# Spreading the gate rows of an mLSTM over all partitions: a DMA from memory in place of a product with a one-hot

## The chip, the cores and the metric

The kernel runs on one core of one Trainium2 chip. The metric is the device time of one execution in microseconds (us); three executions of the kernel before took 1901.86, 1902.31 and 1902.44 us, so its median is 1902.31 us. The engines are TensorE (PE, with its weight loads listed apart as PEld), VectorE (DVE), ScalarE (ACT), GpSimd (POOL) and SyncE (SP), which here only calls transfers.

## The reference, cut to what matters

One layer works on 256 latent tokens and 256 context tokens of width 2048. After a modulated norm, one input projection makes the inputs of three mixers (a gated MLP, a two-way mLSTM, a pooling), an output projection follows, and then a retrieval network over 16,384 experts. The mLSTM has 4 heads of width 256 and runs once forward and once backward. For each head and direction it needs this, for every pair of a query token t and a key token s:

```
log_w = where(causal, b[t] - b[s] + i[s], -inf)
inter = b + m
m_t   = maximum(inter, log_w.max(-1))
w_prev = exp(inter - m_t)
s     = (q k^T) * exp(log_w - m_t)
num   = s v + w_prev * (C q);   den = s.sum(-1) + w_prev * (n q)
h     = num / maximum(|den|, exp(-m_t))
```

Two rows of 256 numbers per head and direction, one for the maximum and one for the weight of the earlier state, are functions of t alone. In the kernel the tokens s lie on the partitions and the tokens t along a row, so both rows have to stand on all 128 partitions before VectorE can combine them with the keys' own numbers.

## The kernel before, in words

All five instruction streams are written out in program order by one Python program; nothing reorders them later. The program walks through a list of units. A unit is half or a quarter of a block of weight columns: SP loads it as float32 (L277), ACT makes its high part `hi` (L295), DVE the rest `lo` (L305), and PE forms 24 products of 256 columns with them (12 of 512 where the tokens are the rows of the result). Three buffers each hold `hi` and `lo`, so ACT and DVE run at most three units ahead of PE. Between two units there stands one unit of the modulation weights (`araw`), which DVE alone multiplies and adds up (L452).

Everything else is written as generators that are resumed from a planner. The planner keeps a clock of PE time (`clock["t"]`, L357): each product adds its estimated time to it. A generator that yields a wait is resumed at the first pause after that wait, counted on this clock, but for the lane `main` not before the planner's own estimates of DVE's and ACT's time plus `MARG` (L327). So the place of a step among the units follows from the sum of the estimates ahead of it, and a product that goes away moves what stands behind it.

The generator `gen_heads` (L786) computes the mLSTM of the latent tokens, while PE works on the units of the o, v, p and u columns. For each head it calls `scores` (4 products, `pS`), and then for each direction `weights`, `products` (10 to 12 products, `num`) and `finish`; `norm` closes the head with a transpose on PE (`hT`, L872). In `weights` (L801) PE forms `bc1`: the transposed one-hot row `ident[:, row]`, read as 36 partitions by 128 columns, times the two rows of all heads in `rows3`, which gives the two rows of this head and direction on all partitions, 512 columns in one of three small PSUM buffers. DVE reads it in three steps (a maximum and a mask), ACT takes the exponential, DVE multiplies the queries by the second row (`qw`) and the weights by the scores (`sT`). The rows in `rows3` are made much earlier by `gen_gates` (L647).

When the last unit is done, `finish_mix` (L978) drains the generators: it runs the rest of `gen_heads` to its end. PE can go on with the output projection only after the last head's `hT` and the split of the mixers' results (`ysplit`). Transfers called by POOL are the row gathers of the retrieval network (L1372), which begin at 757 us.

Of the kernel before, what the change touches and what calls it, by code (L numbers as in the profile page):

```python
# [23 lines left out]
F32 = mybir.dt.float32  # L24
# [8 lines left out]
P = 128  # L33
D = 2048
KD = D // P
T = 256
# [3 lines left out]
HEADS = 4  # L40
# [142 lines left out]
def build(tc, a, stack, dbg=None):  # L183
    nc = tc.nc
    ten, pool, sync = nc.tensor, nc.gpsimd, nc.sync
# [11 lines left out]
    def dump(name, ap):  # L197
        if dbg is not None and name in dbg:
            sync.dma_start(dbg[name], ap)
# [9 lines left out]
    def sm_ps(name="sm"):  # L209
        return psp.tile([P, 512], F32, name=name, tag="sm", bufs=3)  # L210
# [9 lines left out]
    ident, iota, selb, iota_p = c1[:, 0:128], c1[:, 128:256], c1[:, 256:256 + BT], c1[:, 288:289]  # L220
# [126 lines left out]
    def mm(out, lhsT, rhs, start, stop, **kw):  # L347
        n = 1
        for x in rhs.shape[1:]:
            n *= x  # L350
        if rhs.dtype == F32:
            t = max(213.0, n * 4 / 2.4)
            if kw.get("tile_position") is not None:
                t /= 3.5
        else:
            t = max(107.0, n / 2.4)
        clock["t"] += t / 1000.0  # L357
        ten.matmul(out, lhsT, rhs, start=start, stop=stop, skip_group_check=True, **kw)  # L358
# [236 lines left out]
    ROWS = 36  # L595
    V = {}
# [30 lines left out]
    def big():  # L627
        return V["B"].tile([P, 2, T], F32, name="big", tag="t512", bufs=BIGB)


    def row_tile(name):
        return V["B"].tile([ROWS, 2, T], F32, name=name, tag="row", bufs=2)

    def prefix(dst, src, op):

        for r0, way in ((0, 1), (32, -1)):
            for i in range(2):
                d, x = dst[r0:r0 + 4, i, ::way], src[r0:r0 + 4, i, ::way]
                if op is OP.add:
                    vec.tensor_tensor_scan(d, ones[r0:r0 + 4, 0:1].to_broadcast([4, T]), x, 0.0, OP.mult, OP.add)  # L640
                else:
                    vec.tensor_tensor_scan(d, x, x, NEG, op, op)

    def gates_done(ps):
        vec.tensor_scalar(V["rowbuf"].rearrange("p i t -> p (i t)"), ps, vecs[:, V_BG:V_BG + 1], None, op0=OP.add)

    def gen_gates():  # L647
        B = V["B"]
        ig, fg = V["rowbuf"][0:ROWS], V["rowbuf"][64:64 + ROWS]
        e = big()  # L650
        act.activation(e[64:100], fg, AF.Abs)
        act.activation(e[64:100], e[64:100], AF.Exp, scale=-1.0)
        act.activation(e[64:100], e[64:100], AF.Ln, bias=1.0)

        lf = row_tile("lf")
        vec.memset(lf, 0.0)
        vec.scalar_tensor_tensor(lf, fg, 0.0, e[64:100], op0=OP.min, op1=OP.subtract)
        yield GY
        bc = B.tile([ROWS, 2, T], F32, name="bcum", tag="b1")
        vec.memset(bc, 0.0)  # L660
        prefix(bc, lf, OP.add)
        g = B.tile([ROWS, 2, T], F32, name="gexp", tag="b2")
        vec.tensor_tensor(g, ig, bc, op=OP.subtract)
        yield GY
        m = row_tile("pre")
        prefix(m, g, OP.max)
        col = B.tile([ROWS, 4], F32, name="gcol")
        vec.memset(col, 0.0)

        for r0, last in ((0, T - 1), (32, 0)):  # L670
            r = slice(r0, r0 + 4)
            vec.tensor_scalar(col[r, 0:1], m[r, 1, last:last + 1], 0.0, None, op0=OP.max)
            vec.tensor_tensor(col[r, 1:2], bc[r, 1, last:last + 1], col[r, 0:1], op=OP.add)
        vec.tensor_scalar(col[:, 2:3], col[:, 0:1], -1.0, None, op0=OP.mult)
        wk = row_tile("wk")
        vec.memset(wk, 0.0)
        yield GY
        act.activation(wk[:, 0], g[:, 1], AF.Exp, bias=col[:, 2:3])
        act.activation(wk[:, 1], g[:, 0], AF.Copy)
        rows3 = V["rows3"]  # L680
        vec.memset(rows3, 0.0)
        yield GY
        for r0 in (0, 32):
            r = slice(r0, r0 + 4)
            vec.tensor_scalar(rows3[r, 0], m[r, 0], col[r, 1:2], None, op0=OP.max)
            act.activation(rows3[r, 1], rows3[r, 0], AF.Exp, bias=col[r, 1:2], scale=-1.0)
            vec.tensor_tensor(rows3[r, 2], bc[r, 0], rows3[r, 0], op=OP.add)
            act.activation(rows3[r, 2], rows3[r, 2], AF.Exp, scale=-1.0)
        yield GY
        pt = sm_ps("gt")  # L690
        for i in range(2):
            for blk in range(2):
                n = 2 * i + blk
                ten.transpose(pt[:, n * ROWS:(n + 1) * ROWS], wk[:, i, blk * P:(blk + 1) * P],
                              ident[0:ROWS, 0:ROWS])
        for blk in range(2):
            n = 4 + blk
            ten.transpose(pt[:, n * ROWS:(n + 1) * ROWS], rows3[:, 2, blk * P:(blk + 1) * P], ident[0:ROWS, 0:ROWS])
        act.activation(V["gtok"].rearrange("p n r -> p (n r)"), pt[:, 0:6 * ROWS], AF.Copy)
        dump("rows3", rows3)  # L700
        yield 2.0


# [65 lines left out]
    def q_done(c):  # L769
        def f(ps):  # L770
            y = conv_silu(ps, c, 1)
            act.activation(y[:, 0], y[:, 0], AF.Silu)
            act.activation(V["qT"][:, c], y[:, 0], AF.Copy, scale=1.0 / 16.0)
            if c == 7:
                spawn("main", gen_heads())
        return f
# [8 lines left out]

    def gen_heads():  # L786
        B, kT, qT, vlat, Ct = V["B"], V["kT"], V["qT"], V["vlat"], V["Ct"]
        rows3, gtok, mask = V["rows3"], V["gtok"], V["mask"]
        hold = {}

        def scores(h):
            pS = sm_ps("pS")
            for blk in range(2):
                for kt in range(2):
                    mm(pS[:, blk * T:(blk + 1) * T], kT[:, 2 * h + kt, blk * P:(blk + 1) * P],
                       qT[:, 2 * h + kt], start=(kt == 0), stop=(kt == 1))
            S = B.tile([P, 2, T], F32, name="S", tag="b0")
            act.activation(S.rearrange("p b t -> p (b t)"), pS, AF.Copy)
            hold["S"] = S

        def weights(h, d):  # L801
            r, row = d * 4 + h, d * 32 + h
            p1 = sm_ps("bc1")
            mm(p1, ident[0:ROWS, row:row + 1].to_broadcast([ROWS, P]), rows3[:, 0:2].rearrange("p i t -> p (i t)"), start=True, stop=True)
            w = big()
            sT = B.tile([P, 2, T], F32, name="sT", tag="sT", bufs=1)
            rng = [(0, T), (P, T)] if d == 0 else [(0, P), (0, T)]
            for blk in range(2):
                t0, t1 = rng[blk]
                gs = gtok[:, 2 + blk, row:row + 1]  # L810
                for tb in range(t0 // P, t1 // P):
                    tt = slice(tb * P, (tb + 1) * P)
                    if tb == blk:
                        vec.scalar_tensor_tensor(w[:, blk, tt], p1[:, tt], gs, mask[:, d],
                                                 op0=OP.max, op1=OP.add)
                    else:
                        vec.tensor_scalar(w[:, blk, tt], p1[:, tt], gs, None, op0=OP.max)
                act.activation(w[:, blk, t0:t1], w[:, blk, t0:t1], AF.Exp, bias=gs, scale=-1.0)
            qw = B.tile([P, 2, T], F32, name="qw", tag="vw", bufs=1)
            for kt in range(2):  # L820
                vec.tensor_tensor(qw[:, kt], qT[:, 2 * h + kt], p1[:, T:2 * T], op=OP.mult)
            for blk in range(2):
                t0, t1 = rng[blk]
                vec.tensor_tensor(sT[:, blk, t0:t1], w[:, blk, t0:t1], hold["S"][:, blk, t0:t1], op=OP.mult)
            return sT, rng, qw

        def products(h, d, sT, rng, qw):
# [28 lines left out]
        def norm(h):  # L856
# [16 lines left out]
            yb = V["yb"][:, 2 * h:2 * h + 2]  # L873
            vec.tensor_tensor(yb, yb, pt.rearrange("p (v t) -> p v t", v=2), op=OP.mult)

        for h in range(HEADS):
            scores(h)
            yield 2.0
            for d in range(2):
                rest = weights(h, d)  # L880
                yield HY1
                pn, den = products(h, d, *rest)
                yield HY2
                finish(h, d, pn, den)
                yield HY0 if d == 0 else HY3
            yield from norm(h)
# [561 lines left out]
    for i2 in range(NK):  # L1448
        for i in LENT:
            row = i * 2048 // NA  # L1450
# [35 lines left out]
    n = 0  # L1486
# [285 lines left out]
```

## Time and profile before

| what | value |
|---|---|
| median of three executions | 1902.31 us |
| profiled execution, its own time | 1904.08 us |
| its span, first to last instruction | 1902.3 us |
| PE busy | 1685.6 us, 89% of the span |
| DVE, ACT, POOL busy | 64%, 36%, 20% |
| the heads' stretch, first `bc` to last `hT` | 343.4 to 515.1 us |
| PE busy between 335 and 505 us | 167.04 of 170 us |

The profile names tiles by the buffer they were first given, so the spread rows read `bc`, `rows3` reads `rows`, the weights `w` read `big`, `h2` reads `h`, and several small tiles of the mixers that lie in one large buffer read `b`. The helper that keeps the planner's time stands at L133 for every DVE and ACT instruction, and nearly every product stands at L358, so groups are told apart by their tiles. A float32 product is recorded as two PE instructions: 8 products `bc` are 16 records. In the rows "x<-y" is a result and what it is computed from, a time in brackets or behind a bar is idle time before, and "<-" names what ended it.

### The profile page before, as it was taken

The page shows a single profiled execution, that of the slowest core. Times are in us where ns is not written, and L with a number is a line of the kernel's source. Part 1 is how long each engine was busy: PE and PEld are TensorE (multiplying, and loading weights), DVE is VectorE, ACT ScalarE, POOL GpSimd, SP SyncE. Part 2 cuts the span into 40 slices and gives each one's busy share as a digit, 9 for nine tenths or more (in the row PEclk, how much of TensorE's full clock was granted, in tenths as well). Part 3 has the DMA queues.
Part 4 walks back from the last instruction along what each step waited for, and adds up shares of the span by engine and source line. Part 5 has one row for each costly group of instructions (what it writes and reads, how often), then busy time and mean ns, then how long its engine had stood idle before and what let it go on. Part 6 is the DMA issues. An engine that isn't in the chain of part 4 may idle for free.

```text
span 1902.3 us, 29266 instructions
## 1 busy us (share of the span) xinstructions
PE 1685.6 (89%) x11536; PEld 1332.2 (70%) x11536; DVE 1224.2 (64%) x2502; ACT 690.4 (36%) x1093; POOL 374.5 (20%) x324
## 2 busy tenths in 40 slices
PE   5899999999898999999999999999987667767775
PEld 3589779878798998998888788888872223222221
DVE  5246868876898679989998687777554323323232
ACT  4235425555543544544444444444421101101010
POOL 0000000000000000322322233233324333333331
PEclk9999999999899999999999999999999998888887
DMA  9976778887698881999999999999989999999997
GB/s 395 396 259 198 256 252 290 276 290 251 216 363 289 291 311 56 421 394 410 407 411 416 366 410 420 420 420 414 407 338 399 421 421 420 421 420 421 421 421 295
DMA packets 115994, 670.67 MB, mean 353 GB/s; under 512 B 12816, under 2 KB 15632, under 8 KB 53264
## 3 DMA queue, kind: packets, MB, share of 16 engines
q1 hardware_dynamic: 69776, 333.24, 47.0%
q0 software_dynamic: 46080, 335.56, 43.0%
q8 instruction: 90, 1.47, 0.3%
q14 instruction: 48, 0.39, 0.1%
HBM read 664.04 MB, written 4.72 MB: 352 GB/s over the span
## 4 chain that ended last, share of the span: by engine, by line
PE 64%; DMA 24%; DVE 5%; issue 5%; ACT 2%; POOL 1%; SPq 0%; POOLq 0%; ACTq 0%; DVEq 0%
PE ups L358 28%; PE mm L358 24%; DMA gath<-in_v_rows,iT 13%; DMA ring<-in_ada 3%; PE adaps L358 2%; DMA hB<-in_v_rows,iT 2%; PE y L358 2%; DVE lo L133 2%; PE yb L358 2%; DMA rawB<-in_v_rows,iT 2%; DMA rawA<-in_v_rows,iT 2%; PE num L358 1%; DMA raw<-in_u_t 1%; PE sm L358 1%; DMA raw<-in_v_rows,iT 1%
## 5 line engine op out<-in xcount | busy, mean ns | idle before, releaser
L358 PE MATMUL ups<-hf,hi 128*128 128x384 f32 x2048 | 599.1, 364 | 0.0
L358 PE MATMUL ups<-hf,lo 128*128 128x192 f32 x2048 | 514.6, 251 | 10.1 <-DVE lo L133 10.0
L358 PEld LDWEIGHTS ups<-hf,hi 128*128 128x128 f32 x2048 | 384.4, 188 | 53.1 <-issue 47.0
L358 PEld LDWEIGHTS ups<-hf,lo 128*128 128x128 f32 x2048 | 391.0, 191 | 15.2 <-DVE lo L133 14.7
L133 DVE TENSOR_TENSOR lo<-rawB,hi 128x1024 fp32r<-128x1024 f32 x146 | 178.3, 1221 | 102.0 <-ACT hi L133 87.2
L133 DVE SCALAR_TENSOR_TENSOR oh<-c,iT,pick 128x128 f32<-128x128 f32 x192 | 55.3, 344 | 286.7 <-PE pick L358 286.7
L133 DVE TENSOR_TENSOR lo<-rawA,hi 128x1024 fp32r<-128x1024 f32 x146 | 178.1, 1221 | 95.8 <-ACT hi L133 90.2
L1372 POOL DMA_INDIRECT W<-in_u_rows,iT x34 | 50.4, 1483 | 873.4 <-ACT hi L133 756.7
L133 ACT ACTIVATE hi<-rawA 128x1024 fp32r<-128x1024 f32 x146 | 154.2, 1056 | 173.2 <-PE mm L358 64.3
L133 ACT ACTIVATE hi<-rawB 128x1024 fp32r<-128x1024 f32 x146 | 154.2, 1057 | 160.3 <-PE ups L358 59.7
L358 PE MATMUL mm<-xL,hi 128*128 128x256 f32 x864 | 180.7, 290 | 6.1 <-ACT xL L133 3.0
L1372 POOL DMA_INDIRECT gath<-in_v_rows,iT x117 | 134.5, 1149 | 253.5 <-PE y L358 129.9
L358 PEld LDWEIGHTS mm<-xL,hi 128*128 128x128 f32 x864 | 144.3, 192 | 16.0 <-issue 7.5
L358 PE MATMUL y<-gath,wA 128*32 128x512 f32 x672 | 102.6, 692 | 59.1 <-DMA gath<-in_v_rows,iT 59.0
L133 DVE SCALAR_TENSOR_TENSOR adacc<-araw,early,adacc 128x1024 f32<-128x1024 f32 x120 | 152.3, 1277 | 0.0
L133 ACT ACTIVATE uA<-uA 128x4 f32<-128x4 f32 x48 | 9.9, 206 | 365.0 <-DVE oh L133 365.0
L358 PE MATMUL mm<-xL,lo 128*128 128x256 f32 x432 | 122.4, 283 | 0.0
L133 ACT ACTIVATE hi<-W 128x1024 fp32r<-128x1024 f32 x78 | 82.6, 1059 | 97.7 <-PE ups L358 93.0
L358 PEld LDWEIGHTS pick<-W,oh 128*128 128x128 f32 x384 | 78.6, 249 | 55.5 <-issue 53.7
L133 DVE TENSOR_TENSOR lo<-W,hi 128x1024 fp32r<-128x1024 f32 x78 | 94.5, 1218 | 18.4 <-ACT hi L133 17.2
L358 PE MATMUL mm<-hf,hi 128*128 128x256 f32 x512 | 98.3, 292 | 6.2 <-ACT hf L133 5.3
L358 PE MATMUL pick<-W,oh 128*128 128x128 f32 x384 | 97.5, 411 | 1.1 <-issue 1.1
(273 smaller groups left out, 2867.1 us busy)
## 6 DMA issues: line engine op xcount, KB each, us to landing
araw<-in_ada SPq DMA_DIRECT2D x128, 512.0 KB
W<-in_u_t SPq DMA_DIRECT2D x39, 1024.0 KB
rawB<-in_u_t SPq DMA_DIRECT2D x35, 1024.0 KB
rawA<-in_u_t SPq DMA_DIRECT2D x34, 1024.0 KB
ring<-in_ada SPq DMA_DIRECT2D x32, 1024.0 KB
raw<-in_u_t SPq DMA_DIRECT2D x19, 1024.0 KB
rawB<-in_wout SPq DMA_DIRECT2D x16, 512.0 KB
rawA<-in_wout SPq DMA_DIRECT2D x16, 512.0 KB
```

The costliest lines, as they stand in the source:

```text
L133: return f(*args, **kw)
L358: ten.matmul(out, lhsT, rhs, start=start, stop=stop, skip_group_check=True, **kw)
L1372: pool.indirect_dma_start(out=g.raw, out_offset=None, in_=tab, in_offset=bass.IndirectOffsetOnAxis(ap=idx, axis=0))
```

## The change

The two rows are written to a scratch tensor in memory as soon as `gen_gates` has made them, and each head and direction gets them back by a transfer that reads one row of 2 KB 128 times, once per partition, into SBUF. Both kinds of transfer are called by POOL. There are two targets, the tile of `rows3` (which nobody needs any more) and a new one, `bc`, used in turn; the call for step n + 2 stands behind the last DVE instruction of step n, and those of steps 0 and 1 at the head of the generator. The product `bc1` goes away, and with it its time on the planner's clock and its PSUM buffer. DVE reads the rows from SBUF.

```
+    rowd = tc.dram_tile([8, 2 * T], F32, name="rows_spill")
...
+        for n, r0 in enumerate((0, 32)):
+            pool.dma_start(rowd[4 * n:4 * n + 4], rows3[r0:r0 + 4, 0:2].rearrange("p i t -> p (i t)"))
         yield 2.0
...
+        def spread_row(n):
+
+            if n < 2 * HEADS:
+                h, d = divmod(n, 2)
+                spread[n] = B.tile([P, 2 * T], F32, name="bc", tag="rows3" if n % 2 else "bc")
+                pool.dma_start(spread[n], rowd[4 * d + h:4 * d + h + 1].to_broadcast([P, 2 * T]))
...
         def weights(h, d):
             r, row = d * 4 + h, d * 32 + h
-            p1 = sm_ps("bc1")
-            mm(p1, ident[0:ROWS, row:row + 1].to_broadcast([ROWS, P]), rows3[:, 0:2].rearrange("p i t -> p (i t)"), start=True, stop=True)
+            p1 = spread.pop(2 * h + d)
...
+            spread_row(2 * h + d + 2)
             return sT, rng, qw
...
+        spread_row(0)
+        spread_row(1)
         for h in range(HEADS):
```

On POOL's queue ten calls now stand ahead of the first gather (`W<-in_u_rows`), with what each waits for in brackets (`DMASW` is an earlier transfer called by POOL, numbered in turn). Before, nothing stood there:

```order
L704 DMA rows_spill<-rows_1065 4x512 [waits Activation_49] x2
L800 DMA bc<-rows_spill 128x512 [waits DMASW0_49,PE_49]
L800 DMA bc<-rows_spill 128x512 [waits DMASW1_49,PE_49,Activation_49]
L800 DMA bc<-rows_spill 128x512 [waits DMASW2_49,DVE_49]
L800 DMA bc<-rows_spill 128x512 [waits DMASW3_49,DVE_49]
```

The first two spreads wait for the spill and for PE and ACT, which have last used `rows3` in `gen_gates`; from the third on each waits for DVE, that is for the step two before it.

On PE, at the end of the input projection, the kernel before has this (`hi_4440` and `lo_4442` are the last unit of the u columns, `hT` the last head's transpose):

```order
L358 MATMUL mm<-xL,lo_4442 128x256
L358 MATMUL num<-vlat,sT 128x257 x2
L358 MATMUL num<-b_1065,qw 128x257
L358 MATMUL num<-Ct,qw 128x257
L358 MATMUL num<-vlat,sT 128x257
L358 MATMUL num<-b_1065,qw 128x257
L358 MATMUL num<-Ct,qw 128x257
L358 MATMUL mm<-xL,hi_4440 128x256 x2
L358 MATMUL mm<-xL,lo_4442 128x256
```

The changed kernel has it like this, with the last unit now called `hi_4442` and `lo_4444`:

```order
L358 MATMUL mm<-xL,hi_4442 128x256 x2
L358 MATMUL mm<-xL,lo_4444 128x256
L358 MATMUL num<-vlat,sT 128x257 x2
L358 MATMUL num<-b_1066,qw 128x257
L358 MATMUL num<-Ct,qw 128x257
L358 MATMUL num<-vlat,sT 128x257
L358 MATMUL num<-b_1066,qw 128x257
L358 MATMUL num<-Ct,qw 128x257
L883 MATMUL hT<-c_68,hs 128x128 x4
```

The last head's products have moved from the middle of the last unit to behind it, directly ahead of the transpose. With the 12 products of half a unit gone from between them, nothing of PE's is left there.

On DVE, the kernel before has this around the last head's second direction (`big<-bc` is the first read of the spread rows, `adacc` the modulation units, `lo_4488` to `lo_4569` weight units of the output projection, `hs` the head's result):

```order
L133 SCALAR_TENSOR_TENSOR big<-bc_4472,early 128x128
...
L133 TENSOR_TENSOR sT<-big,S 128x256
L133 TENSOR_TENSOR lo_4488<-rawB,hi_4486 128x1024
L133 TENSOR_TENSOR b_2395<-b_2395,mixed 128x256
L133 SCALAR_TENSOR_TENSOR adacc<-araw_4329,early,adacc 128x1024
L133 TENSOR_TENSOR lo_4523<-rawB,hi_4521 128x1024
L133 SCALAR_TENSOR_TENSOR adacc<-araw_4362,early,adacc 128x1024
L133 TENSOR_TENSOR den<-den,early 128x2
...
L133 TENSOR_TENSOR lo_4569<-rawA,hi_4567 128x1024
L133 TENSOR_TENSOR b_2395<-b_2395,mixed 128x256
L133 SCALAR_TENSOR_TENSOR adacc<-araw_4410,early,adacc 128x1024
L133 SCALAR_TENSOR_TENSOR hs<-num,den,hs 128x256 x2
```

In the changed kernel the same place reads:

```order
L133 TENSOR_TENSOR lo_4479<-rawB,hi_4477 128x1024
L133 TENSOR_TENSOR b_2398<-b_2398,mixed 128x256
L133 SCALAR_TENSOR_TENSOR adacc<-araw_4322,early,adacc 128x1024
L133 SCALAR_TENSOR_TENSOR big<-bc,early 128x128
...
L133 TENSOR_TENSOR sT<-big,S 128x256
L133 TENSOR_TENSOR lo_4526<-rawB,hi_4524 128x1024
L133 SCALAR_TENSOR_TENSOR adacc<-araw_4367,early,adacc 128x1024
L133 TENSOR_TENSOR lo_4558<-rawA,hi_4556 128x1024
L133 TENSOR_TENSOR b_2398<-b_2398,mixed 128x256
L133 SCALAR_TENSOR_TENSOR adacc<-araw_4401,early,adacc 128x1024
L133 TENSOR_TENSOR den<-den,early 128x2
...
L133 SCALAR_TENSOR_TENSOR hs<-num,den,hs 128x256 x2
```

The weights' step stands one unit later (one `lo`, one product with `mixed` and one `adacc` have come ahead of it), and `den` has moved behind the third unit; `hs` follows the same three units as before. From the transpose on, the order of PE, DVE, ACT and SP is as it was.

## Rows read from the trace of the kernel before

**Rows 1.** The page: the span, and the chain that ended last by engine.

```profile
span 1902.3 us, 29266 instructions
PE 64%; DMA 24%; DVE 5%; issue 5%; ACT 2%; POOL 1%; SPq 0%; POOLq 0%; ACTq 0%; DVEq 0%
```

**Rows 2.** Busy us by stretch, then clock, DMA share, GB/s; the sum covers 335–505.

```profile
sum 170.00, PE 167.04 PEld 143.67 DVE 132.55 ACT 98.19 POOL 0.00; mean PE 9.83 PEld 8.45 DVE 7.80 ACT 5.78 POOL 0.00
...
402.00:431.00 29.00, 26.92 (x130) 21.24 (x131) 23.50 (x42) 17.18 (x27) 0.00 (x0) 1.00 0.74 237
506.00:514.00 8.00, 0.69 (x7) 0.49 (x5) 4.37 (x10) 4.42 (x11) 0.00 (x0) 0.70 0.87 269
517.00:521.00 4.00, 4.00 (x27) 4.00 (x26) 4.00 (x13) 1.63 (x5) 0.00 (x0) 0.69 0.00 0
```

**Rows 3.** Instructions on tile bc: ns min/median/max, first and last start.

```profile
L358 PE MATMUL bc<-rows,c x16: 589/640/693, 343.4 to 497.1; 36*128 36x512 f32 x16
```

**Rows 4.** Chain of waits in the heads' stretch: start, us, what.

```profile
343.44 1.05 PE bc L358 x2
...
401.97 1.06 ACT hi L133
...
410.76 0.78 DVE big L133 x3
411.54 0.66 DVE qw L133 x2
412.20 0.54 DVE sT L133 x2
...
430.15 0.72 PE hT L872 x4
...
449.54 1.05 PE bc L358 x2
...
496.62 1.05 PE bc L358 x2
```

**Rows 5.** Chain of waits at the end of the stretch.

```profile
505.22 1.32 PE mm L358 x11
...
507.69 1.23 DVE lo L133
508.92 0.34 DVE b L133
509.25 1.19 DVE adacc L133
510.45 0.41 DVE hs L133
...
513.94 1.18 PE hT L872 x4
```

**Rows 6.** Groups of 335–505 us: busy us, mean ns, idle before.

```profile
L133 DVE SCALAR_TENSOR_TENSOR adacc<-araw,early,adacc 128x1024 f32<-128x1024 f32 x40 | 51.1, 1278 | 0.0
L133 DVE TENSOR_TENSOR lo<-rawB,hi 128x1024 fp32r<-128x1024 f32 x21 | 25.7, 1223 | 13.3 <-ACT hi L133 13.0
L133 DVE TENSOR_SCALAR hs<-num,den 128x256 f32<-128x256 f32 x8 | 3.5, 476 | 0.1
L133 DVE TENSOR_SCALAR hs<-hs,hrs 128x256 f32<-128x256 f32 x6 | 1.9, 351 | 0.1
...
L133 DVE TENSOR_TENSOR den<-den,early 128x2 f32<-128x2 f32 x7 | 1.1, 160 | 4.8 <-ACT den L133 4.8
```

**Rows 7.** Longest of the waits in 335–525 us: total, times, longest.

```profile
ACT hi L133 <- PE mm L358: 25.9, 19, 2.4
```

**Rows 8.** The last writer of rows3.

```profile
L133 ACT ACTIVATE rows<-rows x2: 401/409/417, 221.7 to 222.6; 4x256 f32<-4x256 f32 x2
```

**Rows 9.** Chain near the program's end: a gather of 1 MB from call to landing.

```profile
1858.27 16.98 DMA gath<-in_v_rows,iT
```

**Rows 10.** POOL's calls of gathers in 760–1400 us, and DVE's splits beside them.

```profile
L1372 POOL DMA_INDIRECT gath<-in_v_rows,iT x36: 932/1775/1947, 798.0 to 1385.6; - x36
...
L133 DVE TENSOR_TENSOR lo<-W,hi x78: 1201/1218/1226, 722.5 to 1097.0; 128x1024 fp32r<-128x1024 f32 x78
```

More of the change, by code (lines that the diff above doesn't have):

```diff
@@ L787, in gen_heads @@
         B, kT, qT, vlat, Ct = V["B"], V["kT"], V["qT"], V["vlat"], V["Ct"]
-        rows3, gtok, mask = V["rows3"], V["gtok"], V["mask"]
-        hold = {}
+        gtok, mask = V["gtok"], V["mask"]
+        hold, spread = {}, {}
+        def spread_row(n):
[3 more added lines that the diff above has]
+                pool.dma_start(spread[n], rowd[4 * d + h:4 * d + h + 1].to_broadcast([P, 2 * T]))
         def scores(h):
```

## Prediction

> **What bounds the kernel now.** I read the chain of waits first, then the busy times by stretch, then the waits. Over the program PE is 64% of the chain, DMA 24% and DVE 5% [rows 1]. The change touches one stretch, the mLSTM heads, from the first product `bc` at 343.44 us to the last head's transpose, which ends at 515.1 us [rows 4, 5]. Up to 505 us PE is the bound there: it is busy 167.04 of 170 us, DVE 132.55 and ACT 98.19 [rows 2], and the longest wait of the stretch is ACT's `hi` waiting for PE to give a buffer back, 25.9 us in 19 times [rows 7]. No wait in that list, down to its smallest entry, is ended by a transfer. At one place the chain leaves PE: from 401.97 to 430.15 us it runs over ACT and DVE [rows 4], and PE is busy only 26.92 of 29 us [rows 2]. At the end, from 506 to 514 us, PE has 0.69 us of work [rows 2], since the last head has to come through DVE and ACT before `hT` can start at 513.94 us [rows 5].
>
> What an earlier end of the stretch is worth is read just behind it. From 517 to 521 us the DMA share is 0.00 [rows 2]: every load that the buffers allow has landed, so no transfer carries an absolute time across this point. Since from there on the order of all engines is as before, the rest, the DMA-bound part included, should simply start earlier. I count a microsecond won here as a microsecond of the program.
>
> **What goes.** Eight float32 products `bc`, each recorded as two instructions of 640 ns that overlap [rows 3]; on the chain each costs 1.05 us, from the first at 343.44 to the last at 496.62 us [rows 4]. The chain holds seven of the eight. The fourth lies in the piece that runs over ACT and DVE, where DVE's reading (`big`) at 410.76 us follows on DVE's own work; PE has 29 − 26.92 = 2.08 us of slack there, so I count that one at nothing (at most 1.05). Seven times 1.05 is **7.35 us**.
>
> **What is added on the queues.** Ten calls on POOL, which is idle through the stretch [rows 2]. The spill waits for ACT's last write into `rows3`, at 222.6 us [rows 8], and spreads 0 and 1 wait for it and for readers of that time, so they are issued some 120 us before 343 us. Spreads 2 to 7 wait for DVE's last step of the row two before and nothing useful is queued behind them on POOL. Their time to land: the trace of before has no spread, and the farthest row upward is a gather of four times the bytes in a saturated queue, 16.98 us from call to landing [rows 9]; downward it is 0. The time they have is shortest between the fourth reading, which starts at 410.76 us and ends 1.98 us later (0.78 + 0.66 + 0.54), and the sixth, whose `bc` starts at 449.54 us [rows 4]: 36.8 us. Even the upper bound is hidden twice over, so I take 0. What hides it is the distance of two steps; eight steps in the 153 us from 343.44 to 496.62 are 22 us apart in the mean, so with one target instead of two the 17 us would no longer fit everywhere. [...] The spreads move 2 MB, which in a stretch with a DMA share of 0.74 to 0.87 [rows 2] and no wait on a transfer costs 0.
>
> **What is changed on DVE.** Three of five readings a step come from SBUF with one tensor input less from PSUM. Nearest rows: a scaling of 256 columns takes 476 ns out of PSUM and 351 out of SBUF [rows 6]; 0.125 us for each of 8 to 24 instructions is at most 3 us of DVE time, which counts only where DVE is on the chain (under 1 us). [...] I take 0.
>
> **What is moved: the end.** The last head's products now come behind the last unit, so I compare from the moment A when the unit before the last two is done (before: 496.62 us, where `bc` starts) to the first `hs`. Before: 510.45 + 0.41 − 496.62 = 14.24 us [rows 4, 5], of which 1.05 is the `bc` already counted, leaving 13.19. After, DVE's list sets it, piece by piece: ACT's `hi` 1.06 [rows 4], `lo` 1.23, product with `mixed` 0.34, `adacc` 1.19, the weights' step 0.78 + 0.66 + 0.54, then twice `lo` 1.23 and `adacc` 1.19, once more 0.34, `den` 0.16 and a reciprocal of the same size [rows 6], `hs` 0.41: with the rest from [rows 4, 5] it is 11.71 us, all but the first on one engine. PE's part, 24 to 48 products of 0.12 us [rows 5] and `num`, fits beside it. This would give 1.48 us. Against it: DVE may reach A late. A unit takes 1.22 + 1.28 = 2.50 us of DVE [rows 6] and 24 × 0.12 = 2.88 us of PE, so it makes up only 0.38 us a unit, and the last head now has six units beside it instead of seven (its scores come one unit later). One unit's DVE work, 2.50 us, is so the bound of a loss: −1.48 to +1.02 us. I take **−0.5**, near the middle.
>
> **Sum.** −7.35 − 0.5 = −7.85 us. The durations are of the profiled execution, 1904.08 us with a span of 1902.3; the 1.8 us around the span do not change, so it would take 1896.2. The median of the runs is 1902.31, and the same difference gives **1894.5 us**. With the bounds (0 to 1.05 for the fourth product, 0 to 1 for DVE, −1.48 to +1.02 for the end, and 2 to 3 us for reordered steps between, about PE's idle time in the stretch, 2.96 us [rows 2]) the case's own range is 1890.5 to 1898.
>
> **Rivals.** *The gain stops at DVE.* The planner puts the steps of heads 1 to 3 half a unit to a unit later, and DVE is 78% busy, more where a head's step meets a unit of 2.50 in 2.88 us. If the chain goes over to DVE from 401.97 us on, only the first three products count, 3 × 1.05 = 3.15 us, and the time is 1899.2. For it: the piece from 401.97 to 430.15 us. Against it: from 431 us to 505 us the chain is back on PE, and three buffers of `hi` and `lo` are 8.6 us of cover.
>
> *DVE is held while POOL writes out the calls.* Place: right behind each step, where DVE has its two-input instructions `sT` and `lo`. Price: POOL's call takes 0.93 to 1.95 us [rows 10]; ten calls that each hold DVE, and through the missing `lo` PE, are 9.3 to 19.5 us, so the time goes to 1903.7 to 1913.9, about 1909. It decides from 0.8 us a call on. Against it: beside POOL's gathers DVE's `lo` has 1201 to 1226 ns, minimum to maximum, while POOL's own call goes from 932 to a median of 1775 ns [rows 10]: it is POOL that waits. [...]
>
> *The rows come late.* It needs a landing of more than 36.8 us, with every late microsecond six times on DVE; nothing in [rows 9] comes near. With 2 us late each the time would be 1894.5 + 12 = 1906.5.
>
> *More than the sum.* The fourth product counts, DVE gains its 1 us and the end its 1.48: −10.9 us, 1891.4. [...]
>
> **Chances.** The sum 0.70; more 0.08; DVE as the bound 0.14; POOL's calls hold DVE 0.06; late rows 0.02. A difference under 0.2%, 3.8 us, can't be told from no change here. Of the sum's 0.70 some 0.66 lies below 1898.5; with the 0.08 and 0.04 of the DVE case that is 0.78 for faster. Same: 0.04 + 0.10 + 0.01 = 0.15. Slower: 0.07. The range for 8 in 10 is 1890 to 1900.
>
> **What would show it.** Right: no `bc` products, PE products back to back where they were, ten calls on POOL of about 1 to 2 us, each spread landed long before `big` starts, DVE's idle time before `big` ended by no transfer; the last `hT` some 8 us earlier, a DMA share of zero again just behind it, and the same shift at the first gather and at the end. Wrong: DVE waiting for `rows_spill`, `lo` above 1.23 us behind a call, PE waiting for `lo` between 343 and 505 us, more than 7.4 us of PE idle before the last `hT`, or a shift at `hT` that is gone by the end.

## The result, and the profile after

The changed kernel takes **1893.04 us** (median of 5 runs, 1888.43 to 1893.96) against 1902.31 us (median of 5, 1900.41 to 1903.1): a ratio of 0.995, 95% interval 0.994 to 0.996. In a second set of runs it was 1891.58 us (1890.27 to 1893.23), ratio 0.9951 (0.9937 to 0.9965), and the kernel before, run there against itself, had 0.9999 (0.9990 to 1.0008). So some 9 to 11 us are gone, where 7.85 were forecast.

The profiled execution of the changed kernel happens to be the fastest of its five, 1888.43 us. Its page (before: [rows 1]):

```profile
span 1886.6 us, 29258 instructions
PE 64%; DMA 23%; DVE 6%; issue 5%; ACT 1%; POOL 1%; SPq 0%; POOLq 0%; ACTq 0%; DVEq 0%
```

That span is 15.7 us shorter than the one before, more than the runs say. To see what the change itself did, the span is cut at events that both kernels have: the first `pS` on the chain, the last `hT`, the first and the last `ups` (the products of the retrieval network; from the first to the last it is 679.5 to 680.5 us in all four). Two executions of each kernel, in us:

| | up to first `pS` | `pS` to last `hT` | `hT` to first `ups` | last `ups` to the end |
|---|---|---|---|---|
| before | 338.07 | 175.87 | 214.7 | 494.2 |
| before, second set | 338.55 | 175.88 | 214.6 | 492.4 |
| after | 335.41 | 166.22 | 214.6 | 490.9 |
| after, second set | 337.40 | 166.23 | 215.2 | 491.1 |

The heads' stretch repeats to 0.01 us and is 9.65 us shorter; what lies ahead of it differs by 2 us between two executions of one program, and what lies behind by nearly as much. So the 9.65 us are the change's, and the rest of the 15.7 us is not told apart from that scatter by these four. The profiles of the experiments below add something to that: the first `pS` starts at 337.72 to 338.55 us in the three kernels without the spill and at 334.97 to 337.40 us in the ten with it. The difference is there already when ACT first writes `rows` (221.4 to 222.2 us against 218.6 to 221.0), which is before POOL's first call; what makes it is open, and the medians, 9.3 and 10.7 us apart, do not show 2 us on top of the stretch. The experiments below are therefore judged by this stretch, from one profile each, and their times stand beside it.

The stretch in the chain of waits (start, us, what), to be laid beside [rows 4]; its start in the kernel before, and then the changed kernel:

```profile
338.07 1.73 PE pS L358 x8
...
340.37 3.07 PE mm L358 x24
```

```profile
335.41 1.73 PE pS L358 x8
337.14 0.57 PE adat L358 x8
337.71 7.39 PE mm L358 x60
345.10 3.04 PE num L358 x14
```

Before, a `bc` of 1.05 us stood at 343.44 us, behind the 24 products of one unit; now 60 `mm` run through to `num`. The end of the stretch, the rows that answer to [rows 5]:

```profile
481.97 9.97 PE mm L358 x83
...
491.97 0.60 ACT hi L133
...
493.73 1.28 DVE adacc L133
495.01 1.14 DVE lo L133
...
496.48 1.20 DVE adacc L133
...
498.05 0.50 DVE hs L133
...
501.63 1.18 PE hT L883 x4
...
503.91 21.11 PE mm L358 x163
```

PE still runs dry: the last product of the units ends at 491.94 us, the last head's `num` at 495.3, and then `hT` comes over DVE and ACT. With PE out of work the granted clock falls, and it comes back later, as before (us, PE busy, granted clock, DMA share, GB/s):

```profile
499.00:500.00 1.00, 0.00 (x0) 1.00 0.93 258
500.00:501.00 1.00, 0.00 (x0) 0.51 0.87 249
...
505.00:506.00 1.00, 1.00 (x6) 0.50 0.00 0
506.00:507.00 1.00, 1.00 (x7) 0.57 0.00 0
507.00:508.00 1.00, 1.00 (x11) 1.00 0.00 0
```

So PE is granted about half of its full clock, 0.50 to 0.57, from 500 to 507 us (in the kernel before 0.50 from 510 to 519 us), and there is a DMA share of 0.00 again behind it, as [rows 2] had it at 517 to 521 us: the whole shift passes on.

The waits of 335 to 525 us (total, times, longest):

```profile
POOL bc L800 <- DVE qw L133: 174.1, 3, 117.2
...
ACT hi L133 <- PE mm L358: 24.9, 17, 2.2
...
PE hT L883 <- DVE hs L133: 8.5, 3, 6.3
```

The longest is POOL's, waiting for DVE to be done with a row before it calls the next: nothing useful stands behind it. ACT's `hi` still waits mostly for PE [rows 7]. In the whole list no wait is ended by a transfer. The instructions on `bc` (ns min/median/max, first and last start), where [rows 3] had PE's:

```profile
L133 DVE SCALAR_TENSOR_TENSOR big<-bc,early x16: 344/347/350, 341.1 to 490.7; 128x128 f32<-128x128 f32 x16
L133 DVE TENSOR_TENSOR qw<-b,bc x16: 417/419/424, 341.8 to 491.3; 128x256 f32<-128x256 f32 x16
L800 POOL DMA_DIRECT2D bc<-rows_spill x8: 538/538/577, 224.5 to 448.2; - x8
L133 DVE TENSOR_SCALAR big<-bc,early x8: 279/280/283, 341.4 to 490.5; 128x128 f32<-128x128 f32 x8
```

### The profile page after: what moved, and what is told of

Read it like the earlier page. It is cut to its first block, busy times and chain, and to the rows that moved or that the text cites. A ratio compares the mean times of both kernels' runs of the same rounds, so it can differ in the third digit from the quotient of the medians.

```text
span 1886.6 us, 29258 instructions
## 1 busy us (share of the span) xinstructions
PE 1678.3 (89%) x11520; PEld 1331.0 (71%) x11520; DVE 1223.2 (65%) x2502; ACT 689.5 (37%) x1093; POOL 379.8 (20%) x334
## 4 chain that ended last, share of the span: by engine, by line
PE 64%; DMA 23%; DVE 6%; issue 5%; ACT 1%; POOL 1%; SPq 0%; POOLq 0%; ACTq 0%; DVEq 0%
PE ups L358 26%; PE mm L358 25%; DMA gath<-in_v_rows,iT 8%; DMA rawB<-in_v_rows,iT 6%; PE adaps L358 3%; DMA rawA<-in_v_rows,iT 2%; PE y L358 2%; DVE lo L133 2%; DMA ring<-in_ada 2%; DMA raw<-in_v_rows,iT 2%; PE yb L358 1%; PE sm L358 1%; PE num L358 1%; DMA raw<-in_u_t 1%; DMA W<-in_u_t 1%
```

## Experiments: the product and the order, taken apart

The change does two things at once: it takes eight products from PE, and, since these no longer count on the planner's clock, it moves the heads' steps. Two kernels do one each. The first takes the products away and keeps the order (its rows of PE, DVE and ACT are those of the kernel before without `bc`):

```diff
         def weights(h, d):
             r, row = d * 4 + h, d * 32 + h
+            clock["t"] += 2 * T * 4 / 2.4 / 1000.0
             p1 = spread.pop(2 * h + d)
```

> The changed kernel, but the planner's clock is still advanced by the time of the product that is gone, so that every step stands among the units where the kernel before has it. Theory 'products': the eight products' time is won, 7.35 to 8.4 us (8 x 1.05, the fourth perhaps hidden), and the end behaves as in before, so the stretch takes 167.5 to 168.5 us and the total is 7.4 to 8.4 below before; the moved order is worth the other 1 to 2 us. Rival 'order': the products' time is slack on PE and the moved order brings the gain; then this is within 2 us of before, stretch 174 us or more.

Measured: 1891.9 us (1889.94 to 1894.35), ratio 0.9952 (0.9938 to 0.9965); stretch 167.12 us (335.65 to 502.77). That is 0.4 us under the range of the theory and far from the rival's 174.

The second is the kernel before with the product left in and taken off the planner's clock:

```diff
-            mm(p1, ident[0:ROWS, row:row + 1].to_broadcast([ROWS, P]), rows3[:, 0:2].rearrange("p i t -> p (i t)"), start=True, stop=True)
+            ten.matmul(p1, ident[0:ROWS, row:row + 1].to_broadcast([ROWS, P]), rows3[:, 0:2].rearrange("p i t -> p (i t)"),
+                       start=True, stop=True, skip_group_check=True)
```

> The kernel before with its product on PE, but the planner's clock is not advanced for it, so that every step stands where the changed kernel has it. Theory 'products': 0 to 2 us below before, from the end alone; stretch 174 to 176 us. Rival 'order': 6 us or more below before, stretch under 170 us.

Measured: 1898.77 us (1896.56 to 1905.5), ratio 0.9990 (0.9979 to 1.0002), which is not told apart from the kernel before; stretch 173.88 us (337.72 to 511.60), 0.1 us under the range of the theory. The controls that ran beside these two are the second-set rows of the table above; what was expected of them:

> The changed kernel, unchanged, profiled a second time. Theory 'products': the stretch from the first pS to the last hT takes 166.2 us within 0.5, the total is 8 to 10.5 us below before, and ahead of the first pS it lies between 335 and 339 us like before. Rival 'elsewhere': again 335.4 us ahead of pS and a last stage 4 us shorter than before's, total 13 us or more below before.

> The kernel before, unchanged, profiled a second time. In the first pair of profiles the stretch from the first pS to the last hT went from 175.87 us (338.07 to 513.94) to 166.22 us (335.41 to 501.63), 9.65 us less; but 2.66 us more were won ahead of it and 4.0 us more behind the start of the last stage, where the program is the same. Theory 'products': only the stretch differs, the rest varies between executions. It expects 175.9 us (within 0.5) for the stretch again, and a time ahead of the first pS and after the first ups that moves by 1 to 4 us for no change of the program. Rival 'elsewhere': the change also shortens the first and last stages, and then they repeat here within 0.5 us of the first profile of before (338.1 us ahead of pS).

Both stretches came as the theory had them; the changed kernel's total is 10.7 us below before, 0.2 us outside its range. Ahead of the first `pS` the kernel before moved by 0.48 us only, which is within the 0.5 us of the rival, and the changed kernel by 2.0; the section on the result has what all profiles show there.

The four stretches side by side, us:

| | order of before | order of after | moved |
|---|---|---|---|
| with the products | 175.88 | 173.88 | −2.00 |
| without | 167.12 | 166.23 | −0.89 |
| products gone | −8.76 | −7.65 | |

Taking the products away is worth 8.76 us in the old order, where seven on the chain were counted at 7.35. The moved order is worth 0.89 us, where 0.5 was counted. My reading at this point was that the fourth product, which the prediction had counted at nothing, costs its 1.05 us after all: 8 × 1.05 = 8.40, near enough to 8.76. That needed a test of its own.

## Experiments: what one product is worth

Three kernels, all in the order of before, keep the product for some steps and read a spread row for the others. The edit against the changed kernel, here with the fourth alone replaced (not shown: `rows3` is kept for the products, there is one target for the rows, and a row is called one step ahead):

```diff
+        KEEP = (0, 1, 2, 4, 5, 6, 7)
...
-            p1 = spread.pop(2 * h + d)
+            if 2 * h + d in KEEP:
+                p1 = sm_ps("bc1")
+                mm(p1, ident[0:ROWS, row:row + 1].to_broadcast([ROWS, P]), rows3[:, 0:2].rearrange("p i t -> p (i t)"), start=True, stop=True)
+            else:
+                p1 = spread.pop(2 * h + d)
+                clock["t"] += 2 * T * 4 / 2.4 / 1000.0
```

> Seven of the eight products stay and the planner's clock counts the eighth as before, so the order of PE, DVE and ACT is that of the kernel before; only the fourth product (second direction of head 1) is replaced by a spread row. From the first pS to the last hT the kernel before took 175.87 and 175.88 us. Theory of the result so far (the product pushes the chain behind it although ACT and DVE are on the chain there): 1.05 us less, 174.82 us. Rival, as the prediction counted it (it lies in PE's slack): 175.87 us. Third: part of it, because DVE's reading from SBUF can start earlier, 174.9 to 175.8.

Measured: stretch **175.83 us** (336.30 to 512.13; 1900.14 us, one run). The kernel before has 175.87 and 175.88: the fourth product is worth 0.05 us. My theory had 174.82 and fell; the prediction's count stands.

The control keeps `KEEP = (0, 1, 2, 3, 5, 6, 7)`:

> The control: the same with the fifth product (first direction of head 2), which lies on a chain of PE alone. Both theories: 1.05 us less than the kernel before from the first pS to the last hT, 174.82 us; if this one gives less too, a product is worth less than its duration on the chain and the eight together have won something else.

Measured: stretch **174.64 us** (335.87 to 510.51; 1899.89 us, one run): 1.24 us less than before. A product on PE's chain is worth more than the 1.05 us that its row shows.

The third keeps only the fourth, `KEEP = (3,)`:

> Only the fourth product stays, in the order of the kernel before; the kernel without any, in the same order, took 167.12 us from the first pS to the last hT. Theory: 168.17 us. Rival (slack): 167.12 us.

Measured: stretch **167.14 us** (336.14 to 503.28; 1890.33 us, one run), against 167.12 without any: 0.02 us. The fourth is free from both sides, and 8.76 us are seven products at some 1.24 us. The chains with all eight and with none, both in the order of before, say the same piece by piece: cut at `num` and `hT`, they differ by 1.25, 1.23, 1.28, 0.05, 1.24, 1.23, 1.23 and 1.25 us from the first product to the eighth.

Where the other 0.20 us of each lie, the chain of the kernel before shows, read one piece further than the prediction read it (`pl` are products of another mixer):

```profile
344.49 4.51 PE mm L358 x36
...
436.42 4.49 PE mm L358 x36
...
450.59 1.63 PE mm L358 x12
452.22 0.86 PE pl L358 x4
453.08 1.43 PE mm L358 x12
...
472.83 2.86 PE mm L358 x24
...
481.89 4.51 PE mm L358 x36
...
497.67 4.51 PE mm L358 x36
```

Each of these runs of `mm` but those at 453.08 and 472.83 us stands right behind a `bc`. Twelve products there take 1.63 us and twelve others 1.43; 36 take 4.49 to 4.51, and 4.30 in the changed kernel's chain at 445.98 us. The 0.20 us are paid by the first product behind, as PE's and its weight load's timeline of the kernel before shows (start, us, engine, operation, the idle time before it in brackets):

```profile
389.36 1.12 PE L358 MATMUL bc<-rows,c 36*128 36x512 f32 x2
390.41 0.50 PE L358 MATMUL mm<-hi,xL 128*128 128x512 f32 x1
390.75 0.39 PE L358 MATMUL mm<-lo,xL 128*128 128x512 f32 x1
```

```profile
388.82 0.19 PEld L358 LDWEIGHTS mm<-hi,xL 128*128 128x128 f32 x1
389.36 0.29 PEld L358 LDWEIGHTS bc<-rows,c 36*128 36x128 f32 x2 [0.35 <-issue]
390.41 0.19 PEld L358 LDWEIGHTS mm<-hi,xL 128*128 128x128 f32 x1 [0.76 <-issue]
390.52 0.19 PEld L358 LDWEIGHTS mm<-lo,xL 128*128 128x128 f32 x1
```

Among these `mm` the weights of the next come in ahead of it, beside the one that runs (the load at 390.52 us for the product at 390.75). Behind `bc` they do not: the load of the first `mm` starts at 390.41 us, with the product itself, after 0.76 us in which the load path was idle; behind each of the eight `bc` the next load comes after the same 0.76 us. Its 0.19 us are the missing 0.20, as far as durations can say; no run here changed the load alone. Nor is `bc` the only product that does it: behind the eight `adat`, whose weights are 128 rows by 32 columns, 24 `mm` take 3.07 us (at 340.37) where 24 elsewhere take 2.86 (at 472.83), and there too the first load starts with its product:

```profile
340.29 0.30 PEld L358 LDWEIGHTS mm<-xL,hi 128*128 128x128 f32 x2 [0.41 <-ACT big L133]
```

The 0.41 us of an idle load path stand behind the `adat` at 240.85, 407.30 and 468.69 us too; at the first two the profile shows nothing that the load waited for.

## Experiments: the rows' way

Is the distance of two steps needed? One target, so that a row is called only when the step before it has been read:

```diff
-                spread[n] = B.tile([P, 2 * T], F32, name="bc", tag="rows3" if n % 2 else "bc")
+                spread[n] = B.tile([P, 2 * T], F32, name="bc", tag="bc")
...
-            spread_row(2 * h + d + 2)
+            spread_row(2 * h + d + 1)
...
         spread_row(0)
-        spread_row(1)
```

> The changed kernel with one target instead of two: the row of step n + 1 is called only behind step n's last reading, so a call has the distance of one step, about 12 to 27 us, instead of 36 us and more. Theory 'hidden': a spread lands within 10 us of its call, so the stretch from the first pS to the last hT stays at 166.2 us within 0.5 and the total within 2 us of the changed kernel. Rival 'late rows': a landing like that of the big gathers, 17 us; then the steps 14 us apart wait 3 to 5 us each and the stretch is 169 us or more.

Measured: 1891.77 us (1889.59 to 1896.22) against 1901.01 us of the kernel before in this and the next three kernels' set, ratio 0.9951 (0.9935 to 0.9966); stretch 166.22 us, to the hundredth that of two targets. One step is distance enough, and a landing of 17 us is not what happens.

Each call three times over, to see what calls cost DVE and how long a spread takes (the rival 'port' of the next two expectations is the prediction's, that POOL's calls hold DVE; by what they would hold it no run shows):

```diff
-                pool.dma_start(spread[n], rowd[4 * d + h:4 * d + h + 1].to_broadcast([P, 2 * T]))
+                for _ in range(3):
+                    pool.dma_start(spread[n], rowd[4 * d + h:4 * d + h + 1].to_broadcast([P, 2 * T]))
```

> The changed kernel with every spread called three times in a row into the same tile: 24 calls and 6 MB instead of 8 and 2 MB; the second and third call wait for the landing of the one before, which shows what a landing takes. Theory 'hidden': a landing is 2 to 6 us, three in a row end within 18 us, ahead of their reading; the stretch stays at 166.2 us within 1, DVE's instructions keep their durations. Rival 'port': 16 more calls of 0.54 us hold DVE, up to 8.6 us, and the stretch is 168 us or more.

Measured: 1891.5 us (1889.73 to 1898.87), ratio 0.9953 (0.9938 to 0.9968); stretch 166.22 us. Its instructions on `bc`, and what POOL waited for (us, times):

```profile
L801 POOL DMA_DIRECT2D bc<-rows_spill x24: 536/536/593, 225.2 to 459.2; - x24
L133 DVE SCALAR_TENSOR_TENSOR big<-bc,early x16: 343/346/349, 342.1 to 491.7; 128x128 f32<-128x128 f32 x16
L133 DVE TENSOR_TENSOR qw<-b,bc x16: 414/418/422, 342.8 to 492.3; 128x256 f32<-128x256 f32 x16
...
  DMA bc<-rows_spill: 85.4, 16
```

Sixteen calls more, twelve of them within the stretch, and neither DVE's durations on `bc` nor the stretch move. In the changed kernel, with eight calls, DVE's `sT` that lie beside a spread's call take 282 to 286 ns (128 columns) and 419 to 426 ns (256 columns), the other `sT` 284 to 289 and 419 to 422. The second and third call of a row wait for the one ahead to land, since they write the same tile: 85.4 / 16 = 5.3 us, with the call's own 0.54 some 5.9 us from call to landing. The twelve waits within the stretch are 3.69 to 6.34 us, in the mean 4.96, so 5.5 us there; the four at 225 to 254 us give 7.0.

The same transfers called by SP, whose queue holds the loads:

```diff
-                pool.dma_start(spread[n], rowd[4 * d + h:4 * d + h + 1].to_broadcast([P, 2 * T]))
+                sync.dma_start(spread[n], rowd[4 * d + h:4 * d + h + 1].to_broadcast([P, 2 * T]))
```

> The changed kernel with the eight spreads called by SP, in its queue of weight loads, instead of POOL. Theory 'POOL is free': POOL's calls hold nobody, so nothing is won; SP's loads behind a call wait for buffers that DVE frees after that step anyway, so the stretch is 166 to 168 us. Rival 'port': POOL's calls of 0.54 us hold DVE; then the stretch gets shorter by up to 6 x 0.54 = 3.2 us, to 163 us.

Measured: 1894.62 us (1890.75 to 1898.61), ratio 0.9959 (0.9947 to 0.9971), and the stretch 2.3 us longer (168.7 us from the first start of `pS` to the last `hT`'s, 166.4 in the changed kernel by the same view). That is outside the theory's 166 to 168 and far from the rival's 163. The interval of its ratio overlaps that of the changed kernel; the chain of waits tells where the 2.3 us are, and the last row how long DVE waited for a row's landing (us, times):

```profile
338.76 0.33 SPq L277
...
339.18 6.54 DMA bc<-rows_spill
...
345.75 0.81 DVE big L133 x3
...
  DMA bc<-rows_spill: 4.1, 1
```

The first row is called at 339.18 us only, behind the loads in SP's queue, where POOL had called it at 224.5 us, and lands at 345.7: now a transfer ends the wait of `big`, for which DVE sits idle for 4.1 us. Up to the first `num` this kernel is 2.25 us behind the changed one, and behind it 0.1 us more. So a late row does show in the stretch.

## Experiment: the last head earlier

With PE idle 6.3 us ahead of the last `hT`, an order in which the heads run earlier might win more. The planner's distances `HY3`, `HY4`, `HY5` go from 6, 3, 2 to 3, 2, 1, and its margin from `MARG` to 0.5 once the heads run:

```diff
-HY5 = 2.0
+HY5 = 1.0
...
-HY3 = 6.0
-HY4 = 3.0
+HY3 = 3.0
+HY4 = 2.0
...
-                    head[0] = max(clock["t"] + wait * WSC, vec.t + MARG, act.t + MARG)
+                    m = 0.5 if lane == "main" and V.get("heads") else MARG
+                    head[0] = max(clock["t"] + wait * WSC, vec.t + m, act.t + m)
...
+        V["heads"] = True
```

> The changed kernel with the heads' steps pulled ahead among the units: HY3, HY4, HY5 3, 2 and 1 instead of 6, 3 and 2, and within the heads a margin of 0.5 instead of 1.5 on the planner's engine estimates. The last hT then stands 48 products ahead of the end of the units instead of behind them. Theory 'end': PE's wait of 6 to 7 us before the last hT goes and the clock does not fall there; 5 to 9 us below the changed kernel, 1883 to 1887 us. Rival 'DVE': the head's work and the units' together are more than DVE can do in the shorter time, so PE waits for hi and lo instead: 0 to 3 us below, or above.

Measured: 1892.75 us (1891.31 to 1896.31), ratio 0.9954 (0.9938 to 0.9970): no better than the changed kernel. The theory 'end' fell, and the rival had it right. The last `hT` comes early, at 490.72 us. The busy times by stretch show where that goes (us, then busy us of PE, PEld, DVE, ACT, POOL with instructions, granted clock, DMA share, GB/s):

```profile
395.00:405.00 10.00, 7.45 (x32) 5.27 (x32) 5.42 (x12) 6.59 (x12) 0.00 (x0) 0.83 0.71 248
...
495.00:505.00 10.00, 5.53 (x34) 5.13 (x33) 10.00 (x18) 6.66 (x19) 0.00 (x0) 0.74 0.89 319
```

The changed kernel in the same two:

```profile
395.00:405.00 10.00, 8.58 (x45) 6.31 (x44) 6.38 (x14) 8.02 (x12) 0.00 (x0) 1.00 0.63 232
...
495.00:505.00 10.00, 2.75 (x12) 2.09 (x11) 6.91 (x18) 6.83 (x23) 0.00 (x0) 0.75 0.77 261
```

From 495 to 505 us PE has twice the work, but now DVE is busy for all of the 10 us, with the `lo` and `adacc` that it put off; PE does one product from 497.3 to 502.1 us and otherwise waits, longest (2.86 us) for DVE's `ysplit`, and the clock falls all the same (0.74). From 395 to 405 us PE is idle for 2.55 us, where the changed kernel has 1.42. From the first `pS` to the first `ups` it is 381.0 us in both kernels. The stall did not go: it moved from `hs` to the `lo` and `adacc` that stand ahead of `ysplit`.

## Why the prediction was right, and where its sizes were off

**The bound.** PE was the bound up to the end of the stretch, and a microsecond won there was one of the program: the stretch gave 9.65 us, the medians 9.3 and 10.7. Right.

**What goes: the step that was mis-sized.** "On the chain each costs 1.05 us" and "Seven times 1.05 is 7.35 us". The number of products was right for the order of before: the fourth is worth 0.05 and 0.02 us, taken out and put in alone. The price was not: the seven cost 1.23 to 1.28 us each, 1.24 for one alone, and all eight 8.76. The step read the product's own row and not the 0.20 us that the product behind it loses; the rows that show it were in the same view.

**What is added on the queues: nothing.** Right, by a wide margin. A spread lands some 5.9 us after its call (5.5 within the stretch), under the bound of 17 us, and three times the calls change nothing. The sign "calls of about 1 to 2 us" was wrong, 0.54 us: the gathers of [rows 10] are indirect transfers, the spreads are direct ones.

**What is changed on DVE.** Taken at 0, and the readings fit. Not three but all five readings a step come out of SBUF now, 40 in eight steps: the one-input reading went from 343 ns to 280, the two two-input ones from 344 to 347 and from 414 to 419. Eight times 63 ns less, sixteen times 3 and sixteen times 5 more: 0.4 us in all. The 0.125 us that [rows 6] showed for a scaling was no guide for instructions with two tensors.

**What is moved: the end.** −0.5 was taken from −1.48 to +1.02; measured −0.89 without the products and −2.00 with them. From the moment A to the end of the first `hs` the kernel without products in the order of before takes 13.00 us (486.69 to 499.69), the changed kernel 12.27 (product 36 of the last 84 ends at 486.28, `hs` at 498.55): −0.73, in the bounds and most of the 0.89. The prediction's 13.19 still held the 0.20 behind `bc`, and its list of 11.71 fell short by 0.56; whether DVE comes late to A by that much is not shown.

Why the moved order is worth 1.11 us more with the products in place, the chain of the kernel with the products in the new order shows at its end:

```profile
500.12 2.41 PE mm L358 x19
...
502.55 0.69 DVE lo L133
...
508.01 0.49 DVE hs L133
```

There PE leaves the chain at 502.53 us and DVE's list sets the first `hs`, so the eighth product, which costs 1.25 us in the order of before, costs 0.07 here (from the last head's first `num` to `hT` 22.76 us with it and 22.69 without), and the fourth 0.11; the other six cost 1.23 to 1.27. In the order that the changed kernel has, six products count and not seven. The 9.65 us are 8.76 for the products and 0.89 for the order, or 2.00 for the order and 7.65 for the products, as one takes the one or the other first.

**The sum** was −7.85; the stretch gave −9.65, of which, counted with the products first, 1.40 are the 7 × 0.20 behind the products and 0.39 the order. The forecast held because both were small beside its range.

**The rivals.** *DVE as the bound* did not come about from 402 us on, where the rival put it; at the end DVE does hide the eighth product in the new order, and the heads put earlier ran into it. *DVE held by POOL's calls*: 24 calls instead of 8 leave the stretch at 166.22 us, and DVE's `sT` beside a call takes at most 4 ns more than elsewhere (426 to 422). What gets longer in this case is POOL's own call of a gather: in the kernel before the calls `gath<-in_v_rows` take 932 to 1947 ns with DVE at work beside them, 934 to 952 with none. The spreads' direct calls take 538 to 577 ns in the changed kernel, with DVE at work beside each. *Late rows*: not here; with SP as the caller the first row is late, DVE waits 4.1 us for it, and the stretch is 2.3 us longer. *More than the sum* had nearly the right size, 1891.4, for wrong reasons: neither the fourth product nor DVE brought it, and the end only 0.39 us more than was taken.

## What to carry to other kernels

What a product cost on PE's chain here was the distance between its neighbours' starts with and without it, 1.24 us, and not the 1.05 us of its own row: read the chain one piece past an instruction, and compare the same work where nothing foreign stands ahead. Judge a small change by a stretch between two events of one engine that repeats to a hundredth; here the end-to-end times of one kernel scatter by 3 to 9 us and could not have told 7.35 from 8.75. Ask which engine ends the wait behind an instruction that goes: the same product was worth 1.24 us on PE's chain and 0.07 where DVE set the end. When a surplus fits a plausible story, take the one instruction out and put it in alone: here the story was wrong, and one profile each showed it.

## What the runs showed of the hardware

- A product of 36 rows in float32 among the split products costs some 1.24 us on PE's chain, 1.05 in its own row and 0.20 in the next one, whose weights are not loaded ahead (the load path is idle for 0.76 us, and the load starts with its product). The 0.20 us stand behind products with weights of 128 rows by 32 columns too (3.07 us for 2.86).
- POOL's direct call of a spread takes 0.54 to 0.58 us, with DVE at work beside each, and 0.54 to 0.59 when each is made three times over, where its indirect gather takes 0.93 to 0.95 us with no DVE work beside it and up to 1.95 with some [rows 10].
- A broadcast read of one 2 KB row to 128 partitions, called three times over, lands some 5.5 us after POOL's call beside the loads of this stretch, and 7.0 at 225 to 254 us.
- Of DVE's readings only the one with a single tensor input got faster out of SBUF, 343 to 280 ns; those with two stayed within 5 ns of what they took with one of them in PSUM.
